# A decoder layer's last norm: where its rows are spread and in which order its tail is finished

## The chip, the cores and the metric

The kernel runs on one core of a Trainium2 chip. A core has TensorE (PE, matrix products into PSUM), VectorE (DVE), ScalarE (ACT), GpSimd (POOL) and SyncE (SP), whose queue here issues every transfer between HBM and the on-chip memory. The metric is device time of one execution in microseconds; the kernel before has a median of 1702.85 us over three runs (1702.12 to 1704.21).

## The reference

256 tokens of width 2048 go through one layer: a mixing sublayer of three attention branches, a layer norm, and a mixture of 32 experts in 8 groups of 4 with two experts for a token. This case concerns the end, the experts and the second norm:

```
for e in range(N_EXPERTS):
    hid = jax.nn.silu(xt @ w1[e]) * (xt @ w3[e])
    out = out + comb[:, e:e + 1] * (hid @ w2[e])
...
x = layer_norm(ALPHA * x + y, ln2_g[l], ln2_b[l])
```

The norm takes mean and variance of a token's 2048 values, scales them by the row `ln2_g` and adds the row `ln2_b`.

## The kernel before, in words

Tokens are routed to slots: every expert has 32 slots, and four experts fill the 128 columns of a product. `moe_round` runs over eight such groups (q = 0 to 7). For a group, PE gathers the tokens (`prepare`), makes the hidden products with w1 and w3 over two halves c of the inner dimension (`hidden`, line 992: order "1" and "3" of c = 0, then of c = 1), ACT applies Silu, DVE multiplies, PE transposes (`ht`, line 1056), and makes the output products `yp`. `combine` copies yp to `yb` and scatters it back to the tokens with two products `cp`, which DVE adds to `acc` (two halves of 128 tokens, c, of four pieces of 512 columns, i).

Weights stream through places of 2 MB (`slots` and `wx`, nine in all: wk, wkk, wg, wx in the profile). `Stream` holds the list of jobs in order; `ready` says whether the next job has a free place, `used` gives places back behind a product and issues what it can. A transfer is issued by the SP queue in the order of the jobs. It waits until the products that read its part of the place are done, and, as the transfers take eight semaphores in turn, until the eighth transfer before it has landed. For the last group, the output weights are loaded in column blocks (`LAST`, kind "n": first 1024 columns in four jobs of two 1 MB transfers, then twice 512 columns in two jobs of four 512 KB transfers), so that all eight jobs lie in places at the same time.

The second norm needs its rows `ln2_g` and `ln2_b` on all 128 partitions. `load_ln2` makes them: PE multiplies a row with ones (`row_bcast`, line 925, tile l2p, 512 columns in two matmuls, 16 in all), ACT copies each tile into `main.ln`, the place wg3, which the column blocks therefore leave out (line 672). It is called behind the last group's hidden products, and its PSUM tiles are those of the hidden products (h1, h3). The tile scheduler orders instructions of an engine by their dependences, so some of it runs inside the last product.

Then a branch on the device (`tc.If(nr > 0)`) picks the long path if an expert has more than 32 tokens, and `fast_tail` otherwise; the runs take `fast_tail`. There `go` makes yp and combines for the column blocks n = 0, 1, 2; `after` adds statistics and multiplies pieces by g2. `prefill` puts b2 into a PSUM tile w by a product with the identity (line 1148). When mean and 1/std are known, PE adds -mean/std times g2 (line 1180) and for two pieces also the scaled piece itself (line 1182, "whole"); DVE finishes the other pieces with `last_op`, ACT copies the whole ones, SP stores each piece. A matmul of 512 columns in float32 shows as two records in the trace.

Of the kernel before, what the change touches and what calls it, by code (L numbers as in the profile page):

```python
# [18 lines left out]
P = 128  # L19
# [30 lines left out]
def hybrid_trunk(ctx: ExitStack, tc: tile.TileContext, xp, xT, memT, w_mem_kv, w_in, gq, gkv, g_kidx, b_kidx,  # L50
# [585 lines left out]
    class Stream:  # L636
# [4 lines left out]


        def __init__(self, first):
            self.i, self.slot, self.free, self.done, self.once = 0, {}, [], set(), set()
            u = []
            for q in range(NQ):
                u += [(k, q, c, e) for c in range(2) for k in "13" for e in range(4)]
                if first and q == NQ - 1:
                    u += [("n", q, k, (n, h)) for n, (_, w) in enumerate(LAST) for k in range(2) for h in range(w // 512)]
                else:  # L650
                    u += [("2", q, k, e) for k in range(2) for e in range(4)]
            if first:
                a, b, c = HALVES
                self.jobs = [(k, h) for k in u[:a] for h in range(2)] + [(k, None) for k in u[a:b]]
                self.jobs += [(k, h) for h in range(2) for k in u[b:c]] + [(k, None) for k in u[c:]]
            else:
                self.jobs = [(k, None) for k in u]
# [7 lines left out]
        def ready(self):  # L665

            k, h = self.jobs[self.i]
            if k in self.slot:
                old = self.slot[k][1]
            else:  # L670
                if k[0] == "n":
                    self.free = [f for f in self.free if f[0] is not self.ln]
                if not self.free:
                    return False
                old = self.free[0][1]
            return old is None or (old, 1 if h is None else h) in self.done
# [251 lines left out]
    def residual(s):  # L928

        gb, bb = (PS["py"].tile([P, 512], F32, name=f"{n}{s}", tag="yp") for n in ("gb", "bb"))  # L930
        row_bcast(gb, 2 * s)
        row_bcast(bb, 8 + 2 * s)
        for c in range(2):
            a = acc[c][:, s * 512:(s + 1) * 512]
            nc.vector.tensor_tensor(tmp.rearrange("t (p j) -> t j p", j=8),
                                    x1n[c][s // 2][:, :, 64 * (s % 2):64 * (s % 2) + 64],
                                    gb.rearrange("t (p j) -> t j p", j=8), ALU.mult)
            nc.vector.tensor_tensor(tmp, tmp, bb, ALU.add)
            nc.vector.scalar_tensor_tensor(a, tmp, ALPHA, a, ALU.mult, ALU.add)
# [5 lines left out]
    def moe_round(ws, first):  # L945
# [20 lines left out]
        def scatter(q, S):  # L966
            Sc = S
            ScT = sct
            tp = (pa.tile([P, 2, P], F32, name="sct0", tag="pa") if first and q == 0 else
                  PS["pm"].tile([P, 2, P], F32, name=f"sct{q}", tag="lt"))  # L970
            nc.vector.tensor_tensor(Sc, S, comb[:, :, 4 * q:4 * q + 4].unsqueeze(3).to_broadcast([P, 2, 4, SLOT]),
                                    ALU.mult)
            for c in range(2):
                nc.tensor.transpose(tp[:, c, :], Sc[:, c].rearrange("p e s -> p (e s)"), ident)
            nc.scalar.copy(ScT, tp)
            return ScT
# [46 lines left out]
        for q in range(NQ):  # L1023
            if first and q == 0:
                h1, h3 = (pa.tile([P, DE], F32, name=f"h{k}0", tag="pa") for k in (1, 3))
                for k4 in range(2):
                    gather(S, k4, g0[k4], 1)
                    gathered(xg, k4, g0[k4])
                hidden(0, 0, "1", xg, h1, 0, 4)
                weights()  # L1030
                for k4 in range(2, 4):
                    gather(S, k4, g0[k4], 0, V)
                    gather(S, k4, g0[k4], 1)
                    gathered(xg, k4, g0[k4])
                    if k4 == 2:
                        hidden(0, 0, "1", xg, h1, 4)
                hidden(0, 0, "3", xg, h3)
                hidden(0, 1, "1", xg, h1)
                hidden(0, 1, "3", xg, h3)
            else:  # L1040
                S = nx
                h1 = PS["phh"].tile([P, DE], F32, name=f"h1{q}", tag="h1")
                h3 = PS["phh"].tile([P, DE], F32, name=f"h3{q}", tag="h3")
                for c in range(2):
                    hidden(q, c, "1", xg, h1)
                    hidden(q, c, "3", xg, h3)
                    if first and c == 0 and q <= 4:
                        residual(q - 1)
            ScT = scatter(q, S)
            nc.scalar.activation(hb, h1, AF.Silu)  # L1050
            nc.vector.tensor_tensor(hb, hb, h3, ALU.mult)
            if first and q == 0:
                psum2()
            tp = PS["pm"].tile([P, 4, P], F32, name=f"ht{q}", tag="lt")
            for k in range(4):
                nc.tensor.transpose(tp[:, k, :], hb[:, k // 2 * 256 + k % 2:(k // 2 + 1) * 256:2], ident)
            nc.vector.tensor_copy(hT, tp)
            if q + 1 < NQ and not (first and q == 0):
                nx = prepare(q + 1)

            def yp_tile(n):
                return PS["py"].tile([P, 512], F32, name=f"yp{q}{n}", tag="yp")

            if first and q == NQ - 1:
                return last_slices(q, hT, ScT, yp_tile, combine)
            yps = [yp_tile(n) for n in range(4)]
            for k in range(2):
                keys = [("2", q, k, e) for e in range(4)]
                wt = [ws.need(x).rearrange("p (j n) -> p j n", j=2) for x in keys]
                for j in range(2):  # L1070
                    for n in range(4):
                        for e in range(4):
                            nc.tensor.matmul(yps[n][32 * e:32 * e + 32, :], hT[:, 2 * k + j, 32 * e:32 * e + 32],  # L1073
                                             wt[e][:, j, n * 512:(n + 1) * 512], start=(k + j == 0), stop=(k + j == 2),
                                             skip_group_check=True)
                ws.used(keys)
                if first and q == 0 and k == 0:
                    nx = prepare(1)
            for n in range(4):
                combine(q, n * 512, 512, yps[n], ScT)  # L1080
# [22 lines left out]
    def load_ln2():  # L1103
        for i, t in enumerate(ln2):
            for s in range(4):
                ps = PS["phh"].tile([P, 512], F32, name=f"l2p{i}{s}", tag="h3" if s % 2 else "h1")
                row_bcast(ps, 16 + 8 * i + 2 * s)
                nc.scalar.copy(t[:, s * 512:(s + 1) * 512], ps)

# [25 lines left out]
    def fast_tail(go):  # L1135
# [7 lines left out]
        def piece(c, i):  # L1143
            return acc[c][:, i * 512:(i + 1) * 512]
# [12 lines left out]
        def after(i, comb_):  # L1157
            if i < 3:
                comb_()
                for c in range(2):  # L1160
                    stats2(c, i * 512, 512)
                    if (c, i) != (1, 2):
                        nc.vector.tensor_tensor(piece(c, i), piece(c, i), g2[:, i * 512:(i + 1) * 512], ALU.mult)
                if i == 0:
                    prefill(0, 0, PS["phh"].tile([P, 512], F32, name="w00", tag="h1"))
                    prefill(1, 0, PS["phh"].tile([P, 512], F32, name="w10", tag="h3"))
                return
            comb_(then=chain)

        go(after)  # L1170
        for c, i in ((0, 1), (0, 2), (1, 1)):
            prefill(c, i, PS["py"].tile([P, 512], F32, name=f"w{c}{i}", tag="yp"))
        for c in range(2):
            V2(nc.scalar.activation(nb2[:, c:c + 1], rs2[:, c:c + 1], AF.Identity, scale=nm2[:, c:c + 1]))
            V2(nc.scalar.activation(dg[:, c], ident, AF.Identity, scale=nb2[:, c:c + 1]))
            if c == 0:
                V2(nc.scalar.activation(dg[:, 2], ident, AF.Identity, scale=rs2[:, 0:1]))
        for c, i in ((0, 0), (0, 1), (1, 0), (0, 2), (1, 1)):
            whole = i and c == 0
            V2(nc.tensor.matmul(ws[c, i], dg[:, c], g2[:, i * 512:(i + 1) * 512], start=False, stop=not whole))  # L1180
            if whole:
                V2(nc.tensor.matmul(ws[c, i], dg[:, 2], piece(c, i), start=False, stop=True))
# [15 lines left out]
        first_op(0, 3)  # L1198
        first_op(1, 3)
        last_op(0, 3)  # L1200
        last_op(0, 0)
        first_op(1, 2)
        last_op(1, 3)
        for i in (1, 2):
            V2(nc.scalar.copy(piece(0, i), ws[0, i]))
            store(0, i)
        last_op(1, 2)
        last_op(1, 0)
        last_op(1, 1)

    ln2 = [main.ln[:, :D], main.ln[:, D:]]
    go = moe_round(main, True)
    load_ln2()


    nr = nc.values_load(nri[0:1, 0:1], min_val=0, max_val=7)
# [70 lines left out]
```

## Time and profile before

| what | value |
|---|---|
| median of three runs | 1702.85 us |
| profiled execution | 1701.77 us, span 1700.0 us |
| PE busy | 1472.8 us (87%) |
| DVE, ACT, POOL busy | 596.2, 465.0, 13.0 us |
| HBM read | 536.95 MB, 317 GB/s over the span |
| mean granted PE clock | 0.925 |

Busy PE is not PE at its peak, since matmuls are pipelined. "Idle before" an instruction is the engine's idle time ahead of it with what ended it; "issue" is time in which the engine waited for nothing that the profile shows. Rows of the timeline merge like instructions and give the start, the length and the count.

### The profile page before, as it was taken

How to read it: one execution, taken by the hardware profiler on the slowest of the kernel's cores; microseconds unless marked ns; L12 is line 12 of the kernel's file. 1: busy time of each engine (PE TensorE's matmuls, PEld its weight loads, DVE VectorE, ACT ScalarE, POOL GpSimd, SP SyncE). 2: the span in 40 equal slices, each digit the busy share in tenths (PEclk: the TensorE clock that was granted, in tenths of full speed). 3: DMA queues.
4: the chain of work that ended last, by engine and by line, in shares of the span. 5: the costliest groups of instructions: out<-in, count | busy, mean ns of one | idle time of the engine just before them, and what ended most of it. 6: DMA issues, size and time to landing. Idle time of an engine off the chain costs nothing.

```text
span 1700.0 us, 23691 instructions
## 1 busy us (share of the span) xinstructions
PE 1472.8 (87%) x9489; PEld 956.8 (56%) x9489; DVE 596.2 (35%) x1126; ACT 465.0 (27%) x873; POOL 13.0 (1%) x24
## 2 busy tenths in 40 slices
PE   9999999999999999997976967877758768768677
PEld 8989989999999998883321222312212213222122
DVE  6656765565454676551120210200200101001004
ACT  5545455676545444441100000000000000000011
POOL 0000000000000000010000000000000000000000
PEclk9999999999999999998987978978979879879779
DMA  7766665555776667949999999999999999999994
GB/s 237 229 187 165 163 164 160 156 156 163 273 265 210 184 186 262 316 148 424 426 427 426 428 427 427 427 428 426 427 428 426 427 427 427 427 427 427 428 404 158
DMA packets 118279, 540.70 MB, mean 318 GB/s; under 512 B 13680, under 2 KB 27792, under 8 KB 93072
## 3 DMA queue, kind: packets, MB, share of 16 engines
q1 hardware_dynamic: 118160, 539.10, 82.8%
q8 instruction: 77, 1.26, 0.3%
q14 instruction: 42, 0.34, 0.1%
HBM read 536.95 MB, written 2.10 MB: 317 GB/s over the span
## 4 chain that ended last, share of the span: by engine, by line
PE 55%; DMA 41%; DVE 1%; ACT 1%; issue 1%; SPq 1%; POOL 0%; ACTq 0%; DVEq 0%; POOLq 0%
DMA wg<-in_w_dram 17%; DMA wk<-in_w_dram 15%; PE ps L202 10%; PE ps L199 10%; PE ps L201 10%; PE h L992 8%; DMA wkk<-in_w_dram 5%; DMA wx<-in_w_dram 4%; PE ps L208 3%; PE ps L207 3%; PE ps L209 3%; PE yp L1073 3%; PE yp L1096 1%; DMA stt<-in_w_o_dram 1%; SPq L704 1%
## 5 line engine op out<-in xcount | busy, mean ns | idle before, releaser
L148 DVE TENSOR_TENSOR wl<-stt,wh 128x512 fp32r<-128x512 f32 (+1 forms) x492 | 333.9, 684 | 264.1 <-ACT wh L147 260.5
L147 ACT CAST wh<-stt 128x512 fp32r<-128x512 f32 (+1 forms) x492 | 300.7, 615 | 311.1 <-PE ps L201 203.8
L992 PE MATMUL h<-wg,xg 128*32 128x512 f32 x912 | 240.4, 702 | 80.2 <-DMA wg<-in_w_dram 80.2
L199 PE MATMUL ps<-xH,wh 128*128 128x256 f32 x1024 | 293.7, 287 | 0.0
L202 PE MATMUL ps<-xH,wl 128*128 128x256 f32 x1024 | 289.7, 283 | 0.8 <-DVE wl L148 0.7
L201 PE MATMUL ps<-xL,wh 128*128 128x256 f32 x1024 | 289.7, 283 | 0.0
L992 PE MATMUL h<-wk,xg 128*32 128x512 f32 x688 | 201.9, 712 | 57.3 <-DMA wk<-in_w_dram 57.3
L199 PEld LDWEIGHTS ps<-xH,wh 128*128 128x128 f32 x1024 | 196.2, 192 | 1.6 <-issue 1.3
L202 PEld LDWEIGHTS ps<-xH,wl 128*128 128x128 f32 x1024 | 196.1, 192 | 1.5 <-DVE wl L148 1.5
L201 PEld LDWEIGHTS ps<-xL,wh 128*128 128x128 f32 x1024 | 196.3, 192 | 0.3
L963 DVE TENSOR_SCALAR xg<-gp,g1n,b1n 128x128 f32<-128x128 f32 x56 | 23.0, 410 | 428.2 <-PE h L992 375.3
L992 PEld LDWEIGHTS h<-wg,xg 128*32 128x32 f32 x912 | 53.1, 126 | 198.0 <-DMA wg<-in_w_dram 108.8
L992 PE MATMUL h<-wkk,xg 128*32 128x512 f32 x208 | 116.9, 718 | 18.3 <-DMA wkk<-in_w_dram 18.3
L992 PEld LDWEIGHTS h<-wk,xg 128*32 128x32 f32 x688 | 44.5, 128 | 148.7 <-DMA wk<-in_w_dram 83.0
L992 PE MATMUL h<-wx,xg 128*32 128x512 f32 x208 | 115.7, 710 | 12.1 <-DMA wx<-in_w_dram 12.1
L960 ACT ACTIVATE xg<-gp,b1n,g1n 128x128 f32<-128x128 f32 x56 | 25.6, 457 | 361.1 <-PE h L992 252.4
L1073 PE MATMUL yp<-wg,yb 128*32 128x512 f32 x368 | 95.8, 597 | 8.3 <-DMA wg<-in_w_dram 8.3
L1073 PE MATMUL yp<-wk,yb 128*32 128x512 f32 x304 | 87.2, 595 | 5.3 <-DMA wk<-in_w_dram 5.3
L1001 DVE COPY yb<-yp 128x512 f32<-128x512 f32 x15 | 10.4, 692 | 196.4 <-PE yp L1073 170.0
L202 PE MATMUL ps<-oH,wl 128*128 128x256 f32 x256 | 72.0, 281 | 0.0
L199 PE MATMUL ps<-oH,wh 128*128 128x256 f32 x256 | 71.7, 280 | 0.0
L201 PE MATMUL ps<-oL,wh 128*128 128x256 f32 x256 | 71.2, 278 | 0.0
(316 smaller groups left out, 1962.1 us busy)
## 6 DMA issues: line engine op xcount, KB each, us to landing
wg<-in_w_dram SPq DMA_DIRECT2D x76, 2048.0 KB, 27.6
wk<-in_w_dram SPq DMA_DIRECT2D x56, 2048.0 KB, 27.6
stt<-in_w_gate_dram SPq DMA_DIRECT2D x192, 256.0 KB, 2.9
wx<-in_w_dram SPq DMA_DIRECT2D x20, 2048.0 KB, 28.1
wkk<-in_w_dram SPq DMA_DIRECT2D x18, 2048.0 KB, 29.2
stt<-in_w_in_dram SPq DMA_DIRECT2D x104, 256.0 KB, 2.9
stt<-in_w_o_dram SPq DMA_DIRECT2D x64, 256.0 KB, 4.7
wk<-in_w_dram SPq DMA_DIRECT2D x14, 1024.0 KB, 10.1
```

The lines of the kernel that those rows point to most:

```text
L147: nc.scalar.copy(h, src)
L148: nc.vector.tensor_tensor(l, src, h.bitcast(F32), ALU.subtract)
L199: nc.tensor.matmul(o, hb, a.H(kt), start=st_ and b % 2 == 0, stop=False, skip_group_check=True)
L201: nc.tensor.matmul(o, hb, a.L(kt), start=False, stop=False, skip_group_check=True)
L202: nc.tensor.matmul(o, lb, a.H(kt), start=False, stop=sp_, skip_group_check=True)
L207: nc.tensor.matmul(o, ha, wh, start=st_, stop=False)
L208: nc.tensor.matmul(o, ha, wl, start=False, stop=False)
L209: nc.tensor.matmul(o, la, wh, start=False, stop=sp_)
L960: nc.scalar.activation(xg[:, kt], gp[:, j], AF.Identity, scale=g1n[:, kt:kt + 1], bias=b1n[:, kt:kt + 1])
L963: nc.vector.tensor_scalar(xg[:, kt], gp[:, j], g1n[:, kt:kt + 1], b1n[:, kt:kt + 1], ALU.mult, ALU.add)
L992: nc.tensor.matmul(h[32 * e:32 * e + 32, :], xg[:, 8 * c + j, 32 * e:32 * e + 32], wt[e][:, j, :], start=(c == 0 and j == 0), stop=(c == 1 ...
L1073: nc.tensor.matmul(yps[n][32 * e:32 * e + 32, :], hT[:, 2 * k + j, 32 * e:32 * e + 32], wt[e][:, j, n * 512:(n + 1) * 512], start=(k + j = ...
```

## The change

`load_ln2` is called in the last group between the hidden products of c = 0 and c = 1. It uses the four PSUM tiles of yp. The place wg3 is left out already for the last group's jobs of c = 1. In the tail, the two bias products of piece 0 come ahead of the output products, in the PSUM tiles of h1 and h3. Piece (0, 2) is finished on DVE, and the one whole piece, (0, 1), comes last.

```
-            self.i, self.slot, self.free, self.done, self.once = 0, {}, [], set(), set()
+            self.i, self.slot, self.free, self.done, self.once, self.ln = 0, {}, [], set(), set(), None
...
-                if k[0] == "n":
+                if self.ln is not None and k[1] == NQ - 1 and (k[0] == "n" or k[2] == 1):
                     self.free = [f for f in self.free if f[0] is not self.ln]
...
                     if first and c == 0 and q <= 4:
                         residual(q - 1)
+                    if first and c == 0 and q == NQ - 1:
+                        load_ln2()
...
-                ps = PS["phh"].tile([P, 512], F32, name=f"l2p{i}{s}", tag="h3" if s % 2 else "h1")
+                ps = PS["py"].tile([P, 512], F32, name=f"l2p{i}{s}", tag="yp")
...
-                if i == 0:
-                    prefill(0, 0, PS["phh"].tile([P, 512], F32, name="w00", tag="h1"))
-                    prefill(1, 0, PS["phh"].tile([P, 512], F32, name="w10", tag="h3"))
                 return
             comb_(then=chain)
 
+        for c in range(2):
+            prefill(c, 0, PS["phh"].tile([P, 512], F32, name=f"w{c}0", tag=f"h{1 + 2 * c}"))
         go(after)
...
-        for c, i in ((0, 0), (0, 1), (1, 0), (0, 2), (1, 1)):
-            whole = i and c == 0
+        for c, i in ((0, 0), (0, 2), (1, 0), (1, 1), (0, 1)):
+            whole = (c, i) == (0, 1)
...
         last_op(0, 3)
-        last_op(0, 0)
         first_op(1, 2)
-        last_op(1, 3)
-        for i in (1, 2):
-            V2(nc.scalar.copy(piece(0, i), ws[0, i]))
-            store(0, i)
-        last_op(1, 2)
-        last_op(1, 0)
-        last_op(1, 1)
+        for c, i in ((0, 0), (1, 3), (0, 2), (1, 2), (1, 0), (1, 1)):
+            last_op(c, i)
+        V2(nc.scalar.copy(piece(0, 1), ws[0, 1]))
+        store(0, 1)
 
     ln2 = [main.ln[:, :D], main.ln[:, D:]]
     go = moe_round(main, True)
-    load_ln2()
```

The SP queue, last jobs of the last group (wg_8128 is the place wg3; L704 loads hidden weights, L697 column blocks), as a difference:

```order
 L704 DMA wg_8127<-in_w_dram 128x4096
-L704 DMA wg_8128<-in_w_dram 128x4096
-L704 DMA wx<-in_w_dram 128x4096
-L704 DMA wk_104<-in_w_dram 128x4096
-L704 DMA wk_105<-in_w_dram 128x4096
-L697 DMA wk_106<-in_w_dram 128x2x1024 x2
+L704 DMA wx<-in_w_dram 128x4096
+L704 DMA wk_104<-in_w_dram 128x4096
+L704 DMA wk_105<-in_w_dram 128x4096
+L704 DMA wk_106<-in_w_dram 128x4096
 L697 DMA wkk<-in_w_dram 128x2x1024 x2
```

The jobs keep their order; each from the c = 1 "3" weights on lies one place further, and wg3 gets none of them.

PE inside the last group's first hidden product (h_11522 is h1 of q = 7), as a difference:

```order
 L992 MATMUL h_11522<-wg_8126,xg 32x512
-L974 MATMUL sct_11683<-ident,S_9128 128x128 x2
+L925 MATMUL l2p_11595<-rows,ident 128x256 x2
+L925 MATMUL l2p_11599<-rows,ident 128x256 x2
+L925 MATMUL l2p_11603<-rows,ident 128x256 x2
+L925 MATMUL l2p_11607<-rows,ident 128x256 x2
+L974 MATMUL sct_11715<-ident,S_9128 128x128 x2
 L992 MATMUL h_11522<-wg_8127,xg 32x512
```

Half of the rows now stand behind the second of four weight blocks; the other half stands behind the first matmul of the following "3" product. Before, PE had this ahead of the branch:

```order
L925 MATMUL l2p_11712<-rows,ident 128x256 x2
L1056 MATMUL ht_11690<-ident,yb 128x128 x4
L925 MATMUL l2p_11700<-rows,ident 128x256 x2
L925 MATMUL l2p_11720<-rows,ident 128x256 x2
L925 MATMUL l2p_11708<-rows,ident 128x256 x2
L925 MATMUL l2p_11716<-rows,ident 128x256 x2
L925 MATMUL l2p_11724<-rows,ident 128x256 x2
L1216 TENSOR_LOAD nri
L1217 COMPARE_AND_BRANCH
```

Now only ht stands between the last hidden product and the load of `nri` for the branch.

PE in the short tail before, around the combines of block n = 0 (w_14468 and w_14470 are w00 and w10):

```order
L1096 MATMUL yp_14483<-wg_8127,yb 32x512 x5
L1006 MATMUL cp_14458<-yb,sct 128x512
L1006 MATMUL cp_14461<-yb,sct 128x512
L1148 MATMUL w_14468<-wg_8128,ident 128x512
L1148 MATMUL w_14470<-wg_8128,ident 128x512
L1006 MATMUL cp_14473<-yb,sct 128x512
L1006 MATMUL cp_14476<-yb,sct 128x512
L1096 MATMUL yp_14483<-wg_8127,yb 32x512 x3
```

And now at the head of the short tail (w_14423 and w_14425 are w00 and w10):

```order
L1213 UNCONDITIONAL_BRANCH
L1150 MATMUL w_14423<-wg_8128,ident 128x512
L1150 MATMUL w_14425<-wg_8128,ident 128x512
L1098 MATMUL yp_14427<-wkk,yb 32x512 x2
L1098 MATMUL yp_14427<-wg_8125,yb 32x512 x2
L1098 MATMUL yp_14428<-wkk,yb 32x512 x2
```

The two products of the bias have left the combines and stand ahead of the first output product.

## Rows read from the trace of the kernel before

**Rows 1.** Chain that ended last, from 1654 us: start us, length us, what

```profile
1654.46 3.59 PE yp L1096 x11
1658.06 2.22 issue
1660.28 8.77 PE yp L1096 x63
...
1670.96 1.72 PE w L1148 x4
...
1679.84 3.60 PE yp L1096 x30
...
1689.57 1.98 PE w L1180 x4
...
1695.88 0.75 DVE acc L1194
```

**Rows 2.** Timeline of PE, 1638.5 to 1661 us: start us, length us, instructions [idle before]

```profile
1640.46 0.74 PE L1056 MATMUL ht<-ident,yb 128*128 128x128 f32 x4
1641.13 2.93 PE L925 MATMUL l2p<-rows,ident 32*128 32x256 f32 x12
...
1647.47 2.07 PE L925 MATMUL l2p<-rows,ident 32*128 32x256 f32 x4 [0.68 <-ACT wg L1108]
...
1656.14 1.91 PE L1096 MATMUL yp<-wk,yb 128*32 128x512 f32 x3
```

**Rows 3.** DMA queues, 1650 to 1661 us: queue: packets, MB, share of 16 engines

```profile
q1 hardware_dynamic: 2014, 3.89, 99.4%
q8 instruction: 2, 0.03, 1.2%
```

**Rows 4.** Timeline of the SP queue, 1570 to 1665 us (issues)

```profile
1579.93 1.75 SPq L704 DMA_DIRECT2D wg<-in_w_dram  x4
...
1602.41 1.31 SPq L697 DMA_DIRECT2D wk<-in_w_dram  x2
1615.16 3.97 SPq L697 DMA_DIRECT2D wkk<-in_w_dram  x2
...
1652.42 10.09 SPq L697 DMA_DIRECT2D wk<-in_w_dram  x8
```

**Rows 5.** DMA issues from 1600, 1614 and 1652 us: KB each, median us to landing

```profile
wk<-in_w_dram SPq DMA_DIRECT2D x2, 1024.0 KB, 31.7
...
wkk<-in_w_dram SPq DMA_DIRECT2D x2, 1024.0 KB, 22.7
...
wk<-in_w_dram SPq DMA_DIRECT2D x8, 512.0 KB, 10.7
```

**Rows 6.** Stretches: length, busy PE PEld DVE ACT POOL, PEclk, DMA share, GB/s

```profile
1600.00:1615.00 15.00, 7.29 (x40) 1.45 (x38) 0.00 (x0) 0.00 (x0) 0.00 (x0) 0.77 1.01 426
...
1650.00:1660.00 10.00, 3.59 (x11) 0.65 (x12) 0.00 (x0) 0.17 (x1) 0.00 (x0) 0.60 1.02 363
...
1665.00:1670.00 5.00, 5.00 (x42) 1.72 (x35) 0.69 (x1) 0.58 (x1) 0.00 (x0) 1.00 0.85 317
```

**Rows 7.** Timeline of PE, 1579 to 1592 us

```profile
1586.56 1.91 PE L992 MATMUL h<-wk,xg 128*32 128x512 f32 x2 [3.86 <-DMA wk<-in_w_dram]
1591.46 1.06 PE L992 MATMUL h<-wk,xg 128*32 128x512 f32 x1 [2.98 <-DMA wk<-in_w_dram]
```

**Rows 8.** Timeline of DVE, 1666 to 1701 us

```profile
1670.14 0.69 DVE L1010 TENSOR_TENSOR acc<-acc,cp 128x512 f32<-128x512 f32 x1 [1.16 <-PE cp L1006]
...
1671.48 0.67 DVE L1010 TENSOR_TENSOR acc<-acc,cp 128x512 f32<-128x512 f32 x1
...
1688.45 1.40 DVE L1189 SCALAR_TENSOR_TENSOR acc<-acc,mv,wg 128x512 f32<-128x512 f32 x2
...
1690.73 0.75 DVE L1194 SCALAR_TENSOR_TENSOR acc<-acc,rs,w 128x512 f32<-128x512 f32 x1 [0.21 <-PE w L1180]
```

**Rows 9.** Timeline of ACT, 1600 to 1701 us

```profile
1667.45 0.58 ACT L1003 COPY yb<-yp 128x512 f32<-128x512 f32 x1 [17.28 <-PE yp L1096]
...
1695.02 0.58 ACT L1205 COPY acc<-w 128x512 f32<-128x512 f32 x1 [1.99 <-PE w L1182]
```

## The prediction

> **What bounds the kernel now.** I read the chain of waits first, from its end backwards, and then the timeline of the stretch where it begins to run on TensorE (PE) instead of on transfers. Up to 1640 us the kernel follows the weight transfers: the stretch from 1600 to 1615 us moves 426 GB/s with all DMA engines busy [rows 6], and the hidden products wait some 3 to 4 us for each 2 MB weight block [rows 7]. From 1654.46 us to the end no transfer is waited for any more. The chain runs through PE's products yp, the combines and the final normalisation [rows 1]. So the question is when PE gets to that chain, and what it has to do on it.
>
> The timeline answers the first part [rows 2]. The transposes ht, which make the last group's products possible, run from 1640.46 to 1641.20 us. Behind them PE still spreads the rows of the second norm (l2p, line 925), in pieces that wait for ScalarE's copies, until 1649.54 us (1647.47 + 2.07). Then it does nothing for 4.92 us (to 1654.46), runs 11 yp records, stops for 2.22 us, and goes on at 1660.28 us [rows 1, 2].
>
> Are those two gaps waits for weights? The first products read a block issued as two 1 MB pieces at 1602.41 us and one issued at 1615.16 us [rows 4]. Landing took 31.7 and 22.7 us [rows 5], so both were there by about 1641.8 us (the second piece of the latter was out by 1615.16 + 3.97 = 1619.13 us). The gaps are not weight waits. Between l2p and yp stands the branch of the If that picks the short tail, and in 1650 to 1661 us the instruction queue moves two packets of 16 KB (0.03 MB) [rows 3]. I take both gaps as code being fetched after the branch: first the page jumped to, then the one after it. The second page is ready 5.82 us after the first product starts (1660.28 - 1654.46).
>
> **The change part by part.** Times are of the profiled execution: 1701.77 us with a span of 1700.0 us, 1.77 us around it, and 1.08 us below the median of 1702.85 us.
>
> *Spreading the norm's rows earlier.* The 16 matmuls and 8 copies move into the middle of the last group's hidden products, where PE waits 3.86 us and 2.98 us for blocks [rows 7]. Their PE time is 12 records in 2.93 us at the faster clock and 4 in 2.07 us at the slower one [rows 2], so 32 records are about 8 to 17 us. They are split into one half before the third block lands and one half while the "3" products wait for three blocks 4.9 us apart (1586.56, 1591.46). The second half waits for ScalarE to copy the first half, which waits for the last "1" product to give up the place, about when that product's other places are loaded again, 1579.93 us [rows 4]. It ends near 1589 us at the worst rate, ahead of the block at 1591.46 us. I cost it at nothing; without that cover it would be up to 8 us. On the chain PE reaches the branch at 1641.20 instead of 1649.54 us: -8.3 us. The fetch gap of 4.92 us stays, as both ends of it move together; its length is bounded by the 2.22 us of the other gap and, if several engines jump together, by twice 4.92 us, so -2.7 to +4.9.
>
> *The place given up.* The last eight hidden blocks and the last eight output blocks now use eight places, not nine. The transfers keep their order, but the fourth block after 1579.93 us is no longer issued at once; it waits until about 1600.3 us. At 1600.3 us some 2.2 blocks are then in flight instead of 3.2, about 10.7 us of work at 4.9 us each. The queue does not run empty. The output blocks after it are held by the limit on open transfers rather than by places: the places are released half by half or quarter by quarter during the products. I take 0; 0 to +5 (one block).
>
> *Two bias products first in the tail.* They are 4 records. In place they cost 1.72 us between the combines [rows 1]. At the head of the tail PE has just sat idle, and the records then go at 0.84 us each (two steps of the products, 1654.46 to 1656.14, with one record in each column group at a time) [rows 1, 2], 3.4 us in all. The code page that starts there holds the same number of instructions, so 4 bias and about 8 yp records (two steps, 1.7 us) run before the next page is needed, 5.1 us of work within the 5.82 us. PE resumes after the same 5.82 us, with 56 yp records left instead of 53: +0.4 us, and 3.4 us as the upper bound, if the second gap is no page.
>
> [...]
>
> Between the combines the 1.72 us go. The third combine finds its buffer read by 1670.83 us (1670.14 + 0.69), just as PE comes; the fourth has to wait for the addition that ends at 1672.15 us [rows 8], with some yp records now put ahead of it. I take -1.3 us of a possible -1.72 (0 at worst).
>
> *The end of the tail.* Five multiplied biases stay, but only one piece, (0,1), is finished wholly on PE; 14 records become 12. From 1689.57 us at 0.43 us each (4 in 1.72 us) [rows 1], the last pair starts 10 records later, at 1693.9 us. VectorE started its first final operation 1.16 us after the matmul that it needed began (1690.73 against 1689.57) [rows 8], so ScalarE's copy starts at 1695.0 and ends at 1695.6 us with its 0.58 us [rows 9]. VectorE now has 10 operations from 1688.45 us, each 0.66 us behind the one before (two take 1.40 us, one 0.75) [rows 8], with one short wait, ending near 1695.2 us. Before, the end was 1695.88 + 0.75 = 1696.63 us [rows 1]. That is -1.0 us; as the eight stores are now closer together I take -0.7 (0 to -1.1).
>
> Sum: -8.3 + 0 + 0.4 - 1.3 - 0.7 = -9.9 us. 1701.77 - 9.9 = 1691.9 us, and by the median 1.08 more: 1693.0 us.
>
> What is late next: the last product yp starts at 1679.84 us now [rows 1], and would start near 1670.6 us. Its blocks are issued in 1652.42 to 1662.5 us and land 10.7 us later at the median [rows 4, 5]; 317 GB/s in 1665 to 1670 us shows the stream just ending there [rows 6]. So the weights arrive barely in time, and anything gained beyond 2 us more would be lost to them.
>
> **The rivals.**
> [...]
>
> *The first products do wait for weights.* The chain names a transfer ahead of them. Then they start at 1654.46 us as now, and only the 1.3 and 0.7 us remain: 1700.8 us. Against it are the landing times above.
>
> *The weights set the end.* If the clock rises early, gains stop where the last block lands, near 1670.4 us, with one step behind it: the last product ends at about 1671.4 instead of 1683.4 us, -12.0 - 0.7, 1690.2 us.
>
> *Slower: the lost place starves the transfers.* With one block less in flight from 1580 to 1630 us the rate would have to fall. It decides from 13.3 us of lost transfer time on (9.9 gained and 3.4 to be seen); at 70% of 426 GB/s over 50 us it would be 15 us of work and more, ending near 1708 us. Against it: before the issue at 1600.27 us little more than three blocks are in flight now, and the rate is full [rows 6].
>
> **How the numbers follow.** Forecast 0.62, the slow clock 0.15, weights at the end 0.09, first products waiting 0.08, starved transfers 0.06. About 0.2%, 3.4 us, is what a measurement can tell from no change. The first three are faster by more than that: 0.86. The fourth is within it: 0.08. The last is slower: 0.06. The range goes from the weights' floor at 1690.2 us to beyond the slow clock: 1690.2 to 1698.4 us.
>
> **What would show it.** In the profile after, the l2p records stand between 1566 and 1590 us, ht is followed by a gap of about 5 us, the bias products start near 1646 us, a second pause ends near 1652 us, ScalarE reads the first product near 1659.5 us, and the last store's source is ScalarE's copy. Hidden products should end at the same time as now. I am wrong if the hidden blocks land later, if the first bias product starts after 1650 us, or if the last product waits on a transfer.

## The result

The changed kernel has a median of 1693.41 us (1692.2 to 1694.4, four runs) where the kernel before has 1703.53 us in the same comparison: a ratio of 0.9941, 95% interval 0.9924 to 0.9958, or 7 to 13 us saved. 1693.0 us was predicted. The two profiled executions stand 8.0 us apart (1701.77 and 1693.73 us, spans of 1700.0 and 1691.9 us), 1.9 us less than the sum that the prediction made against the profile. So the close hit of the medians is in part luck, and the steps have to be looked at one by one.

The profile after begins as before. The rows of the norm are now spread where TensorE (PE) waits for weight blocks:

```profile
1568.38 3.71 PE L925 MATMUL l2p<-rows,ident 32*128 32x256 f32 x16
1579.39 3.28 PE L925 MATMUL l2p<-rows,ident 32*128 32x256 f32 x14
1583.58 0.69 PE L925 MATMUL l2p<-rows,ident 32*128 32x256 f32 x2
1587.02 1.25 PE L992 MATMUL h<-wk,xg 128*32 128x512 f32 x2 [2.75 <-DMA wk<-in_w_dram]
1591.93 1.06 PE L992 MATMUL h<-wk,xg 128*32 128x512 f32 x1 [3.66 <-DMA wk<-in_w_dram]
```

PE still waits for the same two blocks behind them [rows 7]: the spreading has cost nothing that shows there. At the end, the chain of waits (start, length, what) reads so, against [rows 1]:

```profile
1641.22 0.76 PE ht L1058 x4
1641.98 6.22 issue
1648.20 3.75 PE w L1150 x4
1651.95 1.31 PE yp L1098 x6
1653.27 0.68 issue
1653.94 7.92 PE yp L1098 x68
...
1663.59 10.64 DMA wk<-in_w_dram
1674.23 0.04 issue
1674.28 1.92 PE yp L1098 x10
...
1676.22 0.59 ACT yb L1003
...
1682.33 4.56 PE w L1181 x10
1686.89 0.87 PE w L1183 x2
...
1687.79 0.59 ACT acc L1205
```

The rows behind ht are gone; the first gap has grown from 4.92 to 6.22 us; the bias products w stand behind it; the second pause has shrunk from 2.22 to 0.68 us and ends 5.74 us after the first product (5.82 before). New is the transfer: the last weight piece is issued at 1663.59 us, lands at 1674.23 us, and the last products wait for it. SyncE's timeline shows when the last three jobs, twelve transfers in all, are issued:

```profile
1645.88 18.25 SPq L697 DMA_DIRECT2D wk<-in_w_dram  x12
```

In [rows 4] the last two of these jobs are the eight issues in wk, which end at 1652.42 + 10.09 = 1662.51 us; the job ahead of them lay in wx. Now the last issue ends at 1664.13 us. So PE starts on the products 6.26 us earlier, but the last weights come no earlier.

ScalarE's copies of the three output blocks, and its copy of the last piece, are good marks for the sums below; [rows 9] has the first and the last of before, and its other two stand first here, from the timeline of before, then those of after:

```profile
1677.21 0.58 ACT L1003 COPY yb<-yp 128x512 f32<-128x512 f32 x1 [9.18 <-PE yp L1096]
1683.46 0.58 ACT L1003 COPY yb<-yp 128x512 f32<-128x512 f32 x1 [5.66 <-PE yp L1096]
```

```profile
1660.25 0.59 ACT L1003 COPY yb<-yp 128x512 f32<-128x512 f32 x1 [39.31 <-PE yp L1098]
1668.84 0.59 ACT L1003 COPY yb<-yp 128x512 f32<-128x512 f32 x1 [8.00 <-PE yp L1098]
1676.22 0.59 ACT L1003 COPY yb<-yp 128x512 f32<-128x512 f32 x1 [6.80 <-PE yp L1098]
1687.79 0.59 ACT L1205 COPY acc<-w 128x512 f32<-128x512 f32 x1 [4.59 <-PE w L1183]
```

From the first product behind the branch to the end, the 8.1 us between the spans divide so: the first product starts 6.26 us earlier (1648.20 against 1654.46); from it to the first copy 12.05 instead of 12.99 us; to the second copy 8.59 instead of 9.76; to the third 7.38 instead of 6.25; from there to the span's end 15.68 instead of 16.54. That is -6.26 - 0.94 - 1.17 + 1.13 - 0.86 = -8.10 us.

### The profile page after: what moved, and what is told of

Same layout as the page of the kernel before. It is cut to its first block, busy times and chain, and to the rows that moved or that the text cites. A ratio compares the mean times of both kernels' runs of the same rounds, so it can differ in the third digit from the quotient of the medians.

```text
span 1691.9 us, 23688 instructions
## 1 busy us (share of the span) xinstructions
PE 1466.0 (87%) x9487; PEld 952.8 (56%) x9487; DVE 596.6 (35%) x1127; ACT 464.8 (27%) x872; POOL 13.0 (1%) x24
## 4 chain that ended last, share of the span: by engine, by line
PE 55%; DMA 41%; DVE 1%; issue 1%; ACT 1%; SPq 1%; POOL 0%; ACTq 0%; DVEq 0%; POOLq 0%
DMA wg<-in_w_dram 15%; DMA wk<-in_w_dram 15%; PE ps L202 10%; PE ps L199 10%; PE ps L201 10%; PE h L992 8%; DMA wkk<-in_w_dram 5%; DMA wx<-in_w_dram 4%; PE ps L208 3%; PE ps L207 3%; PE ps L209 3%; PE yp L1075 3%; PE yp L1098 1%; DMA stt<-in_w_o_dram 1%; PE g L953 1%
## 5 line engine op out<-in xcount | busy, mean ns | idle before, releaser
L992 PE MATMUL h<-wg,xg 128*32 128x512 f32 x896 | 229.6, 700 | 76.2 <-DMA wg<-in_w_dram 76.0
L992 PE MATMUL h<-wk,xg 128*32 128x512 f32 x704 | 197.5, 697 | 60.0 <-DMA wk<-in_w_dram 60.0
L992 PE MATMUL h<-wx,xg 128*32 128x512 f32 x208 | 111.3, 687 | 12.0 <-DMA wx<-in_w_dram 12.0
L1075 PE MATMUL yp<-wk,yb 128*32 128x512 f32 x304 | 90.7, 595 | 7.6 <-DMA wk<-in_w_dram 7.6
L1001 DVE COPY yb<-yp 128x512 f32<-128x512 f32 x15 | 10.4, 692 | 192.2 <-PE yp L1075 173.8
```

Of the source, the lines that this page charges most:

```text
L992: nc.tensor.matmul(h[32 * e:32 * e + 32, :], xg[:, 8 * c + j, 32 * e:32 * e + 32], wt[e][:, j, :], start=(c == 0 and j == 0), stop=(c == 1 ...
```

## The experiments

Differences of time are the ratio's times the median of before in the same comparison (1701.1 to 1703.5 us), with the interval. The gap column is counted from the start of the last group of PE records ahead of the branch that waited for another engine (ht; where the rows still follow ht, the last four l2p).

| run | time against before, us | let go to first product | to first copy | to second | to third |
|---|---|---|---|---|---|
| before | 0 | 6.99 | 12.99 | 9.76 | 6.25 |
| changed | -10.1 (-12.9 to -7.2) | 6.98 | 12.05 | 8.59 | 7.38 |
| e1_rows | -5.1 (-7.1 to -3.1) | 7.01 | 12.41 | 10.14 | 6.25 |
| e2_tail | -2.4 (-3.9 to -0.9) | 6.90 | 12.13 | 9.00 | 6.27 |
| e3_hold | +1.5 (0 to +3.1) | 7.04 | 11.11 | 9.77 | 6.24 |
| e6_bias_back | -5.8 (-8.2 to -3.6) | 6.93 | 13.51 | 10.14 | 6.27 |
| e7_pad | -8.0 (-10.4 to -5.8) | 6.79 | 10.35 | 9.38 | 9.17 |
| e8_busy | -8.0 (-10.2 to -5.6) | 6.91 | 12.18 | 8.57 | 6.29 |
| e11_load_early | -9.9 (-12.3 to -7.7) | 6.98 | 12.01 | 8.58 | 7.05 |
| e10_less_after | -9.5 (-11.9 to -7.3) | 6.84 | 11.82 | 8.59 | 6.27 |
| e4_nobranch_after | -7.1 (-9.4 to -4.8) | none | | 9.83 | 11.68 |
| e5_nobranch_before | -7.7 (-10.0 to -5.3) | none | | 11.02 | 10.77 |
| e9_less_nobranch | -11.1 (-13.3 to -8.7) | none | | 11.34 | 7.00 |

**One part at a time: e1_rows.**

```
-        for c in range(2):
-            prefill(c, 0, ...)          # back between the combines
...                                      # and the old order of the last pieces
```

> The changed kernel with the tail put back as it was (bias products between the combines, the old order of the last pieces); the norm's rows stay early, the place stays given up. My theory (the rows went off the chain, the gaps before and in the first products are code being fetched after the branch): about 6.5 us less than the kernel before (5 to 8 us), around 1696 us; first product near 1648 us, 11 records, then a second pause of about 2 us that ends 5.8 us after the first product's start. Rival that the gaps are waits for weights: the first product stays near 1654 us and the time within 1 us of the kernel before.

1696.1 us; the first product at 1648.97 us, then five rows of the timeline with nine records, a pause of 2.74 us and the next product at 1654.45 us, 5.48 us behind the first. The gain is at the lower end of what was expected. The profile names a transfer (wx) as what ended the first gap; e4 below shows that the same products can run without it.

**The other part: e2_tail** (the kernel before with the change's tail alone; some of its lines).

```
+        for c in range(2):
+            prefill(c, 0, ...)
         go(after)
...
+        for c, i in ((0, 0), (1, 3), (0, 2), (1, 2), (1, 0), (1, 1)):
+            last_op(c, i)
```

> The kernel before with the tail's change alone: bias products first, pieces in the new order; the norm's rows stay where they were, just before the branch. My theory (the second pause is a code page, so the bias products lie in time that PE would have waited): 1.6 us less than the kernel before (0.5 to 2.5 us), the second pause shrinks to under 1 us and ends about 5.8 us after the first bias product's start. Rival (no page there; nothing hides the bias products): 3.4 us more at the head less 1.3 and 0.7 us later, so 1.4 us slower.

1698.8 us, 2.4 us faster, where the rival said slower. The second pause is 1.08 us and ends 6.25 us after the first bias product, both a little more than I expected. The two parts add up to -7.5 us, within the interval of the whole.

**The bias products alone: e6_bias_back.**

```
+                if i == 0:
+                    prefill(0, 0, ...)
+                    prefill(1, 0, ...)
                 return
...
-        for c in range(2):
-            prefill(c, 0, ...)
```

> The changed kernel with only the two bias products put back between the first and the later combines; the new order of the last pieces stays. My theory (second pause is a code page, and the last product then waits for the last weights, which land near 1674 us): the second pause grows from 0.7 to about 2 us and ends 5.7 us after the first product's start; the products gain nothing, the combines lose 1.2 to 1.7 us, of which the wait for the last weights (1.1 us) hides a part: 0.5 us slower than the changed kernel (0 to 1.5). Rival (no page there): 3.4 us less work at the head of the tail, of which some 1.5 us are left after the combines: about 1.5 us faster than the changed kernel, if the weights let it.

1695.0 us: 1.6 us above the changed kernel by medians, 4.3 us by ratios, whose intervals overlap. The second pause grows to 2.86 us, as the page theory wants. But I had said that the products gain nothing, and they lose 1.5 us: 13.51 instead of 12.05 us to the first copy. The busy time and granted clock (the number before the last two) of 2 us stretches tell why, first this kernel, then the changed one:

```profile
1652.00:1654.00 2.00, 2.00 (x12) 0.49 (x8) 0.00 (x0) 0.00 (x0) 0.00 (x0) 0.50 1.05 389
1654.00:1656.00 2.00, 2.00 (x13) 0.53 (x9) 0.00 (x0) 0.00 (x0) 0.00 (x0) 0.50 1.06 382
1656.00:1658.00 2.00, 2.00 (x20) 0.64 (x16) 0.00 (x0) 0.00 (x0) 0.00 (x0) 0.83 1.00 345
```

```profile
1650.00:1652.00 2.00, 2.00 (x6) 0.46 (x7) 0.00 (x0) 0.00 (x0) 0.00 (x0) 0.50 1.05 374
1652.00:1654.00 2.00, 1.32 (x10) 0.13 (x14) 0.00 (x0) 0.00 (x0) 0.00 (x0) 0.85 1.01 366
1654.00:1656.00 2.00, 2.00 (x20) 0.62 (x24) 0.00 (x0) 0.00 (x0) 0.00 (x0) 1.00 1.03 379
```

A step is four yp records, one in each column group, which overlap (in e6 two start at 1651.74 and two at 1651.75 us, and all four are over 1.08 us later). Behind the second pause, e6 makes five steps at 0.85 us each, 1651.74 to 1656.02 us, at a granted clock of 0.50; the changed kernel makes all of them at 0.43 us, from 1653.94 us on, with 1.00 granted from 1654 us. Those five steps cost 2.1 us. In the changed kernel the clock is at 0.50 under the bias products (1650 to 1652 us). In all six traces with bias products first and the branch in place (changed, e2, e7, e8, e11 and e10 below) a step takes 0.43 us from the second or third on, and the granted clock is 1.00 from 1652 us (e8, e10, e11), 1654 us (changed, e7) and 1662 us (e2) on; of the four without (before, e1, e3, e6) three make some steps behind the second pause at 0.85 us, with 0.50 granted (before in 1662 to 1664, e1 in 1654 to 1656, e6 in 1652 to 1656 us). The fourth, e3, makes all of them there at 0.43 us (granted clock 1.00 from 1660 to 1664 us) after a pause of 2.06 us. So the bias products and the higher clock went together, but the runs do not show that they alone bring it.

**The place alone: e3_hold.**

```
-                if k[0] == "n":
+                if self.ln is not None and k[1] == NQ - 1 and (k[0] == "n" or k[2] == 1):
```

> The kernel before with one thing changed: the place that the norm's rows take over is given up from the second half's last hidden blocks on, as in the changed kernel; rows and tail as before. My theory: the time of the kernel before within 1 us, hidden products ending at most 1 us later. Rival (one block less in flight starves the transfers): the hidden products end 1 to 5 us later and the time follows, 1 to 5 us slower.

1702.1 us, a ratio of 1.0009 (1.0000 to 1.0018), which both allow. The hidden products end 0.9 us later in its trace than in that of before, as in the trace after; but over the traces that moment varies by 3 us (1638.4 to 1641.7 us), so this row alone proves nothing. A cost of 0 to 3 us is what can be said; my 0 was its lower edge.

**Is it the branch? e4_nobranch_after and e5_nobranch_before.** Both leave out the branch and with it the long path.

```
-    nr = nc.values_load(nri[0:1, 0:1], min_val=0, max_val=7)
-    with tc.If(nr > 0) as cmp:
...
-    with cmp.Else():
-        fast_tail(go)
+    fast_tail(go)
```

> The changed kernel without the branch: the value that it tests is not loaded, and the short tail follows at once. It leaves out the long path for experts with more tokens than places. My theory (both gaps are code being fetched after the branch, and the last weights land near 1674 us whatever PE does): PE's gap of 6.2 us behind ht and the pause of 0.7 us go, the first products then run some 6 us earlier, but the last output product waits for its weights, so only 1 to 3 us of it are left: about 1691.5 us. Rival (the gaps are waits for weights or for other engines): the gaps stay, the time within 1 us of the changed kernel.

> The kernel before without the branch; the long path for experts with more tokens than places is left out. My theory: the 4.9 us gap behind the norm's rows and the 2.2 us pause in the first products go, 5 to 7 us faster than the kernel before, around 1696.5 us. Rival (waits for weights): the first products start as late as before, the time within 1 us of the kernel before.

Both gaps are gone. In e4 PE goes from ht to the bias products and the first output products without a stop, and those products, which "waited" for wx in e1's trace, run at 1642.56 us:

```profile
1640.17 0.74 PE L1058 MATMUL ht<-ident,yb 128*128 128x128 f32 x4 [0.85 <-DVE yb L1053]
1640.75 1.88 PE L1150 MATMUL w<-wg,ident 128*128 128x512 f32 x4
1642.56 0.62 PE L1098 MATMUL yp<-wkk,yb 128*32 128x512 f32 x2
```

They read wkk and wg; the output products first read the block wx, which was named, at 1657.0 us there. In e5 the first output product runs between the rows, 9 us earlier than in the kernel before:

```profile
1645.43 1.05 PE L1096 MATMUL yp<-wk,yb 128*32 128x512 f32 x2
```

The instruction queue fits. In the kernel before it moves one packet of 16 KB in 1651 to 1652 us, ahead of the end of the first gap (1654.46), and one in 1657 to 1658 us, ahead of the end of the second (1660.28); in the changed kernel one comes in 1645 to 1646 us, ahead of 1648.20. Each of these three stretches has this line:

```profile
q8 instruction: 1, 0.02, 6.8%
```

The packets ahead of the first products start at 1651.75 us before and at 1645.51 us in the changed kernel: 4.28 and 4.29 us after PE is let go, 2.71 and 2.69 us ahead of the first product. In e4 there is none from 1640 to 1660 us, where only the weights' queue moved anything:

```profile
q1 hardware_dynamic: 3263, 7.54, 102.6%
```

What fills the 4 us ahead of the packet isn't shown.

The kernel before gains 7.7 us (5 to 7 expected), in part because the output products now also run while the rows wait for ScalarE's copies. The changed kernel gains nothing that can be measured, where 1 to 3 us were expected: -7.1 us against before, where e7, in the same comparison, has -8.0. It runs the first products 6 us earlier and then waits for the last block piece by piece:

```profile
1667.55 2.39 PE L1098 MATMUL yp<-wk,yb 128*32 128x512 f32 x12 [0.31 <-DMA wk<-in_w_dram]
1670.22 1.04 PE L1098 MATMUL yp<-wk,yb 128*32 128x512 f32 x2 [0.28 <-DMA wk<-in_w_dram]
1671.57 1.04 PE L1098 MATMUL yp<-wk,yb 128*32 128x512 f32 x2 [0.31 <-DMA wk<-in_w_dram]
1672.88 1.90 PE L1098 MATMUL yp<-wk,yb 128*32 128x512 f32 x10 [0.27 <-DMA wk<-in_w_dram]
```

**Is the second pause the next page of code? e7_pad** (40 small products, 80 instructions with their weight loads, far ahead of the branch, in time that PE waits anyway; nothing reads their results).

```
                         load_ln2()
+                        wt_ = PS["pm"].tile([P, P], F32, name="pad", tag="lg")
+                        for _ in range(40):
+                            V2(nc.tensor.matmul(wt_, ones, ones, start=True, stop=True))
```

> The changed kernel with 40 small dummy products (80 instructions of PE) put behind the rows' spreading in the last group, where PE waits for a weight block, so that the tail's instructions lie further back in PE's program by 80; they compute nothing that is used. My theory (the second pause is the crossing into the next code page after the branch): the place of the crossing moves: the pause of 0.7 us comes at another record than the seventh yp or disappears among the products, while the gap of about 6 us before the first bias product stays; the time is that of the changed kernel within 1 us. Rival (the pause belongs to the seventh yp record, a wait for a weight piece): it stays at the seventh yp record.

The gap before the first product stays (6.05 us), and the pause of 0.68 us is gone. The chain runs through 74 yp records without a stop:

```profile
1643.35 6.04 issue
1649.39 3.75 PE w L1151 x4
1653.14 9.01 PE yp L1101 x74
1662.15 2.62 PE cp L1006 x6
1664.77 11.54 DMA wk<-in_w_dram
1676.31 0.04 issue
1676.35 1.92 PE yp L1101 x10
```

So the pause hangs on where the instructions lie, not on the seventh yp record or on its data. The first copy comes 1.7 us sooner behind the first product than in the changed kernel, and the third copy gives it back: 9.17 us behind the second, with the last piece landing at 1676.31 us.

**Why did the gap grow? e8_busy and e11_load_early.** The gap of 6.2 us stood against my 4.92. Counted from the start of ht, the first product comes after 6.98 us; counted from the start of the last l2p group before [rows 2], 1654.46 - 1647.47 = 6.99 us.

```
     go = moe_round(main, True)
+    for c in range(2):
+        t = PS["phh"].tile([P, 512], F32, name=f"busy{c}", tag=f"h{1 + 2 * c}")
+        V2(nc.tensor.matmul(t, ident, ln2[1][:, :512], start=True, stop=True))
```

> The changed kernel with two dummy products of the bias products' size (3.75 us of PE at the slower clock) behind the last ht, ahead of the branch; nothing reads them. In six of the traces so far the first product behind the branch starts 6.8 to 7.0 us after the START of the last group of PE records that had to wait for another engine (ht, or the last l2p), whatever that group itself takes. My theory now: PE's instruction stream runs ahead of the array, so the way through the branch starts when that group is let go: the first bias product still starts about 7.0 us after ht's start, the idle gap shrinks to some 2.5 us, and the time is that of the changed kernel within 1 us. Rival, as in my prediction (the gap begins when PE's work ends): the gap stays above 5 us, the first bias product starts about 10.7 us after ht, and the time is 2 to 3.7 us longer.

```profile
1640.26 0.74 PE L1058 MATMUL ht<-ident,yb 128*128 128x128 f32 x4 [0.85 <-DVE yb L1053]
1640.85 1.88 PE L1212 MATMUL busy<-wg,ident 128*128 128x512 f32 x4
1647.17 3.75 PE L1150 MATMUL w<-wg,ident 128*128 128x512 f32 x4 [4.45 <-issue]
1650.86 1.60 PE L1098 MATMUL yp<-wkk,yb 128*32 128x512 f32 x2
1653.01 0.59 PE L1098 MATMUL yp<-wkk,yb 128*32 128x512 f32 x1 [0.56 <-issue]
```

6.91 us from ht's start, with the idle gap down to 4.45 us. The dummies took 1.88 us instead of the 3.75 I had reckoned with, so the gap is larger than the 2.5 us expected. By the rival the first product would have started at the dummies' end plus 6.2, 1648.9 us; it started at 1647.17. So the 7 us of the way through the branch run from the moment PE is let go (6.91 us here, 6.98 without the dummies), not from the end of its work. The time, -8.0 us, can't be told from the changed kernel's. This run also moves the second pause: with four more records ahead of the branch it stands behind two yp records instead of six, so it follows the place in the code, as in e7.

```
                         load_ln2()
+                        R["nr"] = nc.values_load(nri[0:1, 0:1], min_val=0, max_val=7)
...
-    nr = nc.values_load(nri[0:1, 0:1], min_val=0, max_val=7)
+    nr = R["nr"]
```

> The changed kernel with one move: every engine loads the value that the branch tests inside the last group, right behind the rows' spreading, not directly ahead of the branch; the branch stays. It divides the 7.0 us between ht's start and the first bias product into the load and the jump. If it is the jump (code being fetched): still 6 us or more. If the load is a good part: 3 to 5.5 us, and the second pause, counted from the first product, is as before 5.7 us after it. Either way the time is that of the changed kernel within 1 us, or up to 1 us less, since the last weights then set the end.

```profile
1640.73 0.75 PE L1059 MATMUL ht<-ident,yb 128*128 128x128 f32 x4 [0.85 <-DVE yb L1054]
1647.71 3.75 PE L1151 MATMUL w<-wg,ident 128*128 128x512 f32 x4 [6.24 <-issue]
```

6.98 us again: loading the value takes no measurable part in the gap. What is left is the branch itself and the way to the code behind it.

**Do the last weights set the end? e9_less_nobranch and e10_less_after.** Both leave out the last 2 MB, and the last slice's second half uses the first half's block, so its result isn't the reference's.

```
-   ... for n, (_, w) in enumerate(LAST) for k in range(2) for h in range(w // 512)]
+   ... for n, (_, w) in enumerate(LAST) for k in range(2) for h in range(w // 512)][:-1]
...
-                 wt["n", q, k, (n, e // ne)][...]
+                 wt["n", q, k if n < 2 else 0, (n, e // ne)][...]
```

> The changed kernel without the branch (and without the long path), and without the last 2 MB of weights: the last slice's second half reads the first half's block again, so the products of that half are not the reference's. If the last weights' landing sets the end once the gaps are gone (my theory): 4 to 5.5 us faster than the kernel without the branch, the last product no longer behind a transfer. Rival (PE and the combines set the end there): within 1 us of the kernel without the branch.

> The changed kernel with its branch, but without the last 2 MB of weights, as in the run without the branch (the last slice's second half reads the first half's block). My theory (with the branch, PE is only just ahead of the weights): the 1.1 us that the third ScalarE copy lost go, 0.5 to 1.5 us faster than the changed kernel, and PE's chain then sets the end. Rival (the weights' landing is the bound here already, by more than that wait): 3 us faster or more.

Without the branch: 1690.25 us, 4.0 us below e4 by medians, 3.9 us by ratios (0.9935, 0.9922 to 0.9949), at the lower edge of the 4 to 5.5 us expected. The third copy comes 31.40 us after ht's start instead of 34.66. The last transfer on the chain now ends at 1662.73 us, ahead of the second block's last products, and the chain has no transfer behind it. With the branch: 1692.2 us (0.9944, 0.9930 to 0.9957), not to be told from the changed kernel. The third copy is 6.27 us behind the second, without a wait; but e8, with all its weights, has 6.29 too, so in time this pair stays inconclusive. It speaks against the rival of 3 us or more without excluding it: by ratios e10 is 0.5 us slower than the changed kernel, and the two intervals together leave some 4 us either way.

None of the runs points to a kernel that would be measurably faster than the changed one: what the gap of 6.22 us and the pause of 0.68 us still cost, the last weights take back.

## Why the prediction was right, point by point

*Spreading the rows earlier: right in kind, too large.* -8.3 us was taken, -6.26 us measured. The failed step is "the fetch gap of 4.92 us stays, as both ends of it move together". Its beginning is the start of the last group that PE's stream waited for. Before, the last l2p group filled 2.07 us of the 6.99 us; ht fills 0.75 us of 6.98, so 1.3 us more of the same 7.0 us show as idle time. The other 0.76 us is a later start of ht (1641.22 against 1640.46 us), less than that moment varies between traces. The -2.7 to +4.9 us of the bounds held the longer gap. That the spreading costs nothing where it now stands was right as far as the waits behind it show.

*Two bias products first: right place, wrong sign.* +0.4 us was taken, and the way to the first copy became 0.94 us shorter. The second pause did end 5.74 us after the start and did hide the bias products. What I missed is the clock: [rows 6] gave 0.60 for 1650 to 1660 us, and I took the share of slow steps as fixed. The kernel before ran behind its second pause at these granted clocks (the number before the last two):

```profile
1660.00:1662.00 2.00, 1.72 (x16) 0.72 (x19) 0.00 (x0) 0.00 (x0) 0.00 (x0) 0.88 0.97 346
1662.00:1664.00 2.00, 2.00 (x12) 0.53 (x8) 0.00 (x0) 0.00 (x0) 0.00 (x0) 0.50 1.05 384
1664.00:1666.00 2.00, 2.00 (x20) 0.73 (x16) 0.00 (x0) 0.00 (x0) 0.00 (x0) 0.77 1.05 388
```

Three of its steps, from 1661.68 us on, took 0.85 us in place of 0.43, some 1.3 us in all; the changed kernel has none of these. From the end of the pause to the first copy it needed 6.31 us instead of 7.17, so the 0.4 us of more work that the prediction reckoned with is in it, too. The slow clock of the prediction's chances is all 14 steps at the 0.84 us of [rows 1, 2]: 11.8 us where 13 took 7.2 us (1660.28 to 1667.45 us [rows 1, 9]), 4.6 us more than the forecast, 1697.6 us. No run shows all 14 at that pace: the changed kernel went the other way, and e6, with five of them at 0.85 us, is the kernel in which it partly happens.

*The page after the branch: borne out as far as the runs go.* The prediction put both gaps down to code being fetched, my reading of two packets [rows 3]. e4 and e5 remove them with the branch, so they were not waits for weights. e11 rules out the load, e7 and e8 move the second one with the place in the code, and a 16 KB packet of the instruction queue starts ahead of the end of each: 2.71 and 2.53 us before, 2.69 and 2.59 us in the changed kernel. What the 4 us between the wait's end and the first packet consist of, no run divides further. The second pause was 2.22 us in [rows 1], 2.86 us in e6 and 0.68 us in the changed kernel. That kernel's next packet, at 1657.83 us, comes without a pause: the chain runs yp from 1653.94 to 1661.86 us.

*The place given up.* 0 us taken; 0 to 3 us by e3, open within that.

*Combines and the end of the tail.* -1.3 and -0.7 us taken, -1.17 and -0.86 us measured.

*What is late next.* "The weights arrive barely in time" was the right warning, but its price was left out of the sum. One of the prediction's own signs of being wrong, that the last product waits on a transfer, came true. Its rows could have shown it: the last issue ended at 1662.5 us and landed 10.7 us later [rows 4, 5], near 1673 us, while the forecast had the last products start at 1670.6 us, and the rival of the weights put the landing at 1670.4. It came at 1674.23 us: the third copy waits 1.13 us in this trace, 0 in e8's, 0.8 in e11's and 2.9 in e7's (against the 6.25 us of before). Too much on the first term, too little on the second and this one: -8.3 + 0.4 was taken for what measured -6.26 - 0.94, the combines and the tail came to the 2.0 us taken for them, and the weights took 1.13 back. The profile pair is 1.9 us short of the sum for that. The median pair happens to lie on it, but its interval of 7 to 13 us holds both, so that agreement is luck.

## What to carry to other kernels

Work that stands between the last wait and a branch on the device can be cheaper than a sum of durations says: here the jump's time ran from the last wait, not from the end of the work (e8: 6.91 us from ht's start, with the dummies' 1.88 us inside). Work that filled the pause behind the jump cost nothing either (12.05 us to the first copy, 13.51 in e6 without it), and here it went together with a higher clock in what followed (1.00 against 0.50 in 1654 to 1656 us). Before costing a gain at the head of a tail, look at when the last transfer lands: the changed kernel waits 1 us for it already, and another 6 us taken out of the gap gave nothing. Take an idle time's named releaser as a hint only: e1's profile named a transfer for products that don't read it, and without the branch the same products ran 6 us earlier.

## What the runs showed of the hardware that I had not expected

The jump on the device took PE 6.8 to 7.0 us from the last wait to the first product behind it in ten traces, and loading the tested value earlier changed nothing in it (6.98 us in e11 and in the changed kernel). In nine of the ten, all but e7, a second pause ended 5.5 to 5.8 us after that product (6.25 us in e2); in the traces of before and of the changed kernel this was 2.53 and 2.59 us after a 16 KB packet of the instruction queue started. 80 more instructions ahead of the branch were enough to make that pause vanish: 0.68 us in the changed kernel, none in e7.
